# The first differential attention part issued head by head behind its own projections

## The chip, the cores and the metric

The kernel runs on one core of one Trainium2 chip. The metric is the device time of one execution in microseconds. A profile is one execution taken by the hardware profiler; its span runs from the first to the last instruction.

## The reference

One layer of a streaming encoder over 2048 prompt tokens and 32 sample tokens of width 1024. What the change touches is the projection and the differential attention of group A (4 heads; two query and key maps of 64 dimensions a head, values of 128):

```python
z = rmsnorm(x, g_attn) @ w_in            # q, k, v of group A, then of group B
s = einsum('bqhmd,bkhmd->bhmqk', q, k) * 64 ** -0.5 + bias[:, None]
p = softmax(where(mask, s, NEG))         # mask: chunks of 64, causal
w = p[:, :, 0] - lam * p[:, :, 1]
oa = einsum('bhqk,bkhe->bqhe', w, v)
```

Group B (8 heads of 64) attends to its own and the previous 8 chunks. Both groups are normed and joined, projected by `w_out` and added to the input. Then follow a squared-ReLU MLP of width 4096, a gate with a per-layer input p, and a final norm. Outputs are the tokens and all new keys and values.

## The kernel before

All matrix products are in fp32 parts: each operand is split into a high and a low part (`split`, L178: ScalarE or VectorE makes the high part, GpSimd or VectorE the low one), and `mm3` (L212) takes three matmuls for each product.

Tokens are handled in four blocks of 512 (the last one with the 32 sample tokens): blocks 0 and 1 are `HALVES[0]`, 2 and 3 `HALVES[1]`. For a block, `prep` (L359) loads the raw tokens, transposes them (tile xp) and makes the operands aH and aL; there is room for two blocks of them. `proj` (L438) computes values (tile vps, in `vtile`) and, for each of four head groups g, first queries and then keys (tile qps): one weight unit of 1024 x 128 (`wunit`, L189), and 24 matmuls for each block. VectorE takes the product out of PSUM (L476 for queries, L481 for keys), ScalarE and GpSimd split it into the tiles qh and ql, each in two buffers, and DMAs write them to HBM as qS and kS. New keys of group A are transposed back (tile ktp, L504), copied (kn) and written to the outputs. `prep_p` (L894) does the same to the per-layer input: transposes (ppt, L911), split into pph and ppl, which share the buffers of qh and ql, and DMAs to pS.

`attn_a` (L572) does attention A for a list js of query pairs (256 tokens each): for each head g it loads the bias tile ba, and a key tile ka with the keys up to the last pair, and calls `attn_a_pair` (L596) for each pair: a load of q, scores (tile s, L638), maximum and exponential (L644 to L652), the difference of the two maps (L674, L675), transposes (tpp, L713) with their split (L720, L721), the value products (tile o, L727 to L729), and the sub-norm (ss, L738). Scores go through three PSUM banks, transposes through two, o through one. The projection has a ring of two banks (pool mm). Pairs 0 to 3 are the first part (`JA0`), pairs 4 to 8 the second (`JA1`, much later). `attn_b` does attention B (scores sb, transposes tpb, products ob).

All DMAs are issued by SyncE (SP) in one line (`dma`, L152, L157). A DMA on SP that has to wait for another engine, or for an earlier DMA, holds those behind it. The order on each engine isn't the order of the calls: the tile framework places the instructions by their priority (the order of the calls, unless `lifted` raises it) and by a simulated time line, so that later work may stand between the instructions of earlier work as far as data, buffers and pools allow. Each engine then runs its own list in order.

In `run` the part around the change is, in the order of the calls: preparation of blocks 0 and 1 with group A's values; the bias tables (`lam`, `biases`); the queries and keys of group A for both blocks and all four heads, woven with `prep_p`, whose transposes and ktp go through the two banks of the attention's transposes; attention A for pairs 0 and 1 of all heads, then for pairs 2 and 3; group B's projection of block 0; that of block 1 woven with the preparation of block 2; attention B for pairs 0 to 3; group B's projection of block 2 woven with the preparation of block 3; and so on.

Of the kernel before, what the change touches and what calls it, by code (L numbers as in the profile page):

```python
# [42 lines left out]
HALVES = [(0, 1), (2, 3)]  # L43
# [29 lines left out]
GS = 3  # L73
OW = 1
KBW = 1184
JA0 = [(0, 1), (2, 3)]
JA1 = [(4, 5), (6, 7, 8)]
JB = [(0, 1), (2, 3), (4, 5), (6, 7, 8)]
ONP = (28, 1, 6)
# [4 lines left out]
def drain(gen):  # L84
    for _ in gen:
        pass
# [13 lines left out]
def weave(main, side, step, i=0, n=1):  # L100
    for _ in main:
        if i % step == 0:
            for _ in range(n):
                next(side, None)
        i += 1
    drain(side)
# [37 lines left out]
class Kern:  # L144
# [424 lines left out]
                    self.qS[gi, ms[0], :, j : j + n].rearrange("r k l c -> r (k l c)"),  # L569
                )  # L570

    def attn_a(self, js, pool, ps_s, ps_t, ps_o):  # L572
        nc = self.nc
        last = 8 in js
        nk = SP if last else 256 * (js[-1] + 1)
        late = []
        for g in range(4):
            ba = self.bias_a(pool, g)
            kt = pool.tile([P, 2, 1024 if self.small else SP], F32R, tag="ka", bufs=2, name="ka")
            if last:  # L580
                ks = pool.tile([P, 2, PAST + SS], F32R, tag="ks", bufs=1, name="ks")
            for hl in range(2):
                src = self.kS[g, hl].rearrange("(m r) c -> r m c", m=2)
                for c0 in range(0, nk, 1024):
                    c1 = min(c0 + 1024, nk)
                    self.dma(kt[64 * hl : 64 * hl + 64, :, c0:c1], src[:, :, c0:c1])
                if last:
                    self.dma(ks[64 * hl : 64 * hl + 64], src[:, :, SP:KC])
            for j in js:
                self.attn_a_pair(g, j if j < 8 else None, kt if j < 8 else ks, ba, pool, ps_s, ps_t, ps_o, late)  # L590
                if self.small:
                    late.pop(0)()
        while late:
            late.pop(0)()
# [861 lines left out]
    def run(self):  # L1456
        tc, nc, a = self.tc, self.nc, self.a
        with ExitStack() as top:

            def opened(stack, name, bufs, space=None, side="left"):  # L1460
                kw = {} if space is None else {"space": space}
                return stack.enter_context(
                    tc.tile_pool(name=name, bufs=bufs, side=side, reuse_waits="tile", **kw)
                )
# [7 lines left out]
            mm = opened(top, "mm", MM, PSUM)  # L1472
            tp = mm
            psx = ExitStack()
            ps_s = opened(psx, "pss", 5 - MM, PSUM, "right")
            ps_t = opened(psx, "pst", 2, PSUM, "right")
            ps_o = opened(psx, "pso", 1, PSUM, "right")
# [3 lines left out]
            sg = opened(s12, "sg", 2)  # L1481
            self.rb = {}
            with ExitStack() as x:
                pp = opened(x, "pp0", 3, side="right")
                wv = opened(x, "wv0", 1, side="right")
                acts = {b: self.actpair() for b in HALVES[0]}
# [15 lines left out]
                for b, i in todo:  # L1502
                    for c in range(2):
                        self.vtile(b, i, 0, c, units[c], acts, sg, mm)
                    next(gen, None)
            ppx = ExitStack()
            pp = opened(ppx, "pp", 1)
            self.rawp = Rings((self.wp, "wr"), (opened(ppx, "wr3", 1), "wr"))
            with ExitStack() as x:
                wk = opened(x, "setup", 1, side="right")  # L1510
                self.lam(cp, wk)
                self.biases(wk, ps_t)
                qk = self.proj(HALVES[0], 0, acts, sg, mm, Rings((ps_t, "tp")), vs=())
                weave(qk, self.prep_p(sg, wk, ps_t), 2)
            self.small = True
            mark = tc.tile_snap_priority()
            with ExitStack() as x:
                pool = opened(x, "a0", 1, side="right")
                for js in JA0:
                    self.attn_a(js, pool, ps_s, ps_t, ps_o)  # L1520
            drain(self.proj((0,), 1, acts, sg, mm, tp))

            def lifted(gen):
# [40 lines left out]
            with ExitStack() as x:  # L1564
                pool = opened(x, "a1", 1, side="right")
# [3 lines left out]
            wk = opened(sq_, "wk", 1)  # L1569
# [47 lines left out]
            wk = opened(top, "wk4", 1, side="right")  # L1617
# [6 lines left out]
            with ExitStack() as x:  # L1624
                act = Sized(opened(x, "acth", 2), BLK, True)
                weave(self.outproj(2, wk, oa[2], md, acc[2]), self.oload(3, wk, act, oa), 1, 0, 2)
                g = self.outproj(3, wk, oa[3], md, acc[3])
# [10 lines left out]
            g = self.gate(0, h, up, None, md, wk, made[0])  # L1638
# [11 lines left out]
            g = self.gate(2, h, up, None, md, wk)  # L1650
# [10 lines left out]
            g = self.gate(3, h, up, cs, md)  # L1661
# [50 lines left out]
```

## Time and profile before

| what | value |
|---|---|
| median of 3 runs | 3154.2 us (3153.26 to 3156.3) |
| span of the profiled execution | 3144.6 us |
| the median less the span | 9.6 us |
| granted TensorE clock over the span | 0.985 |
| TensorE busy | 3011.4 us, 96% |
| VectorE, ScalarE, GpSimd busy | 60%, 60%, 59% |

The profiled execution has no time of its own in the results; its span is set beside the median, and what lies around the span is taken to be 9.6 us. In the profile PE is TensorE's matmuls, PEld its weight loads, DVE VectorE, ACT ScalarE, POOL GpSimd and SP the queue of DMA issues. Matmuls overlap, so that the busy time of PE is a union of overlapping records. A row of a stretch gives its length, each engine's busy time with the count of its instructions, the granted clock, the mean busy share of the 16 DMA engines, and GB/s. A row of a wait gives who waited for whom, the total, how often, and the longest.

### The profile page before, as it was taken

The page shows a single profiled execution, that of the slowest core. Times are in us where ns is not written, and L with a number is a line of the kernel's source. Part 1 is how long each engine was busy: PE and PEld are TensorE (multiplying, and loading weights), DVE is VectorE, ACT ScalarE, POOL GpSimd, SP SyncE. Part 2 cuts the span into 40 slices and gives each one's busy share as a digit, 9 for nine tenths or more (in the row PEclk, how much of TensorE's full clock was granted, in tenths as well). Part 3 has the DMA queues.
Part 4 walks back from the last instruction along what each step waited for, and adds up shares of the span by engine and source line. Part 5 has one row for each costly group of instructions (what it writes and reads, how often), then busy time and mean ns, then how long its engine had stood idle before and what let it go on. Part 6 is the DMA issues. An engine that isn't in the chain of part 4 may idle for free. (4 is left out here: it accounts for less than half of the span.)

```text
span 3144.6 us, 52811 instructions
## 1 busy us (share of the span) xinstructions
PE 3011.4 (96%) x17913; PEld 2649.6 (84%) x17913; DVE 1897.6 (60%) x4596; ACT 1878.1 (60%) x4166; POOL 1847.6 (59%) x2496
## 2 busy tenths in 40 slices
PE   8999898999999999999999999999899999999998
PEld 7787786899977887878788888878788887999998
DVE  5157774645465654666756556535667885576653
ACT  6257775766676764776666656554555455554545
POOL 2357455332345644665655545667877888667674
PEclk9999999999999999999999999999999999999999
DMA  8788757986788746555564543437533446333231
GB/s 281 244 244 244 204 185 229 263 232 201 205 250 230 218 130 153 152 154 153 157 184 130 144 123 103 145 116 241 179 128 115 144 152 229 123 107 107 88 116 56
DMA packets 523287, 539.27 MB, mean 171 GB/s; under 512 B 38749, under 2 KB 401569, under 8 KB 523017
## 3 DMA queue, kind: packets, MB, share of 16 engines
q1 hardware_dynamic: 523016, 535.89, 57.5%
q8 instruction: 142, 2.33, 0.3%
q14 instruction: 129, 1.05, 0.1%
HBM read 421.97 MB, written 117.75 MB: 172 GB/s over the span
## 5 line engine op out<-in xcount | busy, mean ns | idle before, releaser
L176 POOL TENSOR_TENSOR wl<-wr,wh 128x256 fp32r<-128x256 f32 x648 | 475.6, 766 | 354.8 <-ACT wh L181 315.7
L181 ACT ACTIVATE piece<-wr 128x512 fp32r<-128x512 f32 x406 | 246.1, 626 | 272.7 <-PE ups L217 113.1
L176 POOL TENSOR_TENSOR piece<-wr,piece 128x256 fp32r<-128x256 f32 x404 | 327.4, 837 | 99.7 <-ACT piece L181 86.4
L181 ACT ACTIVATE wh<-wr 128x1024 fp32r<-128x1024 f32 x228 | 241.2, 1058 | 171.7 <-PE qps L217 40.7
L166 POOL TENSOR_TENSOR wl<-wr,wh 128x256 fp32r<-128x256 f32 x264 | 199.4, 787 | 194.1 <-ACT wh L181 183.9
L216 PE MATMUL dps<-uh,piece 128*128 128x272 f32 (+1 forms) x768 | 247.0, 325 | 7.5 <-ACT piece L181 3.2
L166 POOL TENSOR_TENSOR piece<-wr,piece 128x256 fp32r<-128x256 f32 x280 | 237.0, 878 | 26.9 <-ACT piece L181 21.5
L218 PE MATMUL dps<-uh,piece 128*128 128x272 f32 (+1 forms) x768 | 247.8, 325 | 1.6 <-POOL piece L166 1.3
L217 PE MATMUL dps<-ul,piece 128*128 128x272 f32 (+1 forms) x768 | 247.8, 323 | 0.0
L216 PE MATMUL ups<-cs,piece 128*128 128x256 f32 (+1 forms) x864 | 246.0, 285 | 1.0 <-DVE r L1232 1.0
L217 PE MATMUL ups<-cs,piece 128*128 128x256 f32 (+1 forms) x864 | 245.3, 284 | 0.0
L218 PE MATMUL ups<-cs,piece 128*128 128x256 f32 (+1 forms) x864 | 245.2, 284 | 0.0
L216 PE MATMUL qps<-aH,wh 128*128 128x512 f32 (+1 forms) x640 | 231.2, 361 | 7.3 <-ACT kn L506 4.0
L218 PE MATMUL qps<-aH,wl 128*128 128x512 f32 (+1 forms) x640 | 229.5, 359 | 0.0
L217 PE MATMUL qps<-aL,wh 128*128 128x512 f32 (+1 forms) x640 | 228.5, 357 | 0.0
L1173 DVE TENSOR_TENSOR h<-h,dps 128x512 f32<-128x512 f32 x256 | 174.3, 683 | 80.9 <-PE dps L218 75.4
L1221 DVE TENSOR_TENSOR h<-h,dps 128x272 f32<-128x272 f32 (+1 forms) x384 | 189.3, 515 | 51.8 <-PE dps L218 50.8
L216 PE MATMUL dps<-uh,wh 128*128 128x512 f32 x512 | 207.8, 406 | 9.4 <-DVE h L1173 5.7
L216 PE MATMUL ups<-cH,wh 128*128 128x512 f32 x512 | 202.8, 396 | 2.1 <-ACT cH L181 1.1
L638 PE MATMUL s<-ka,q 128*128 128x512 f32 (+3 forms) x768 | 187.2, 345 | 15.9 <-ACT e L652 7.1
L218 PE MATMUL dps<-uh,wl 128*128 128x512 f32 x512 | 201.7, 394 | 0.5 <-POOL wl L166 0.4
L217 PE MATMUL ups<-cL,wh 128*128 128x512 f32 x512 | 201.2, 393 | 0.0
(317 smaller groups left out, 9634.2 us busy)
## 6 DMA issues: line engine op xcount, KB each, us to landing
wr<-w_up SPq DMA_DIRECT2D x128, 512.0 KB, 4.0
wr<-w_down SPq DMA_DIRECT2D x128, 512.0 KB, 3.8
wr<-w_in SPq DMA_DIRECT2D x74, 512.0 KB, 5.1
q<-qS SPq DMA_DIRECT2D x128, 256.0 KB, 5.4
v<-vSa SPq DMA_DIRECT2D x64, 512.0 KB, 3.9
ka<-kS SPq DMA_DIRECT2D x32, 512.0 KB, 8.9
wr<-w_out SPq DMA_DIRECT2D x32, 512.0 KB, 4.7
wr<-w_ple_gate SPq DMA_DIRECT2D x32, 512.0 KB, 4.3
```

The source lines that it names most:

```text
L166: nc.gpsimd.tensor_tensor(out[:, sl], a[:, sl], b[:, sl], op=op)
L176: nc.gpsimd.tensor_tensor(out[:, sl], a[:, sl], b[:, sl], op=op)
L181: nc.scalar.activation(hi, raw, AF.Copy)
L216: nc.tensor.matmul(ps, lh, rh, start=start and i == 0, stop=False)
L217: nc.tensor.matmul(ps, lh, rl, start=False, stop=False)
L218: nc.tensor.matmul(ps, ll, rh, start=False, stop=stop and i == n - 1)
L638: nc.tensor.matmul(s, q[:, m, hl, P * qi : P * qi + nr], kt[:, m, k0 - kb : k0 - kb + n], start=hl == 0, stop=hl == 1)
L1173: nc.vector.tensor_tensor(hv, hv, ps, op=ALU.add)
L1221: nc.vector.tensor_tensor(hv, hv, ps, op=ALU.add)
```

## The change

Queries and keys of group A are no longer projected for all heads first. For each head g, `run` calls the projection of that head's queries and keys for both blocks, woven with two of the eight steps of `prep_p`, and then attention A of that head for the pairs 0 to 3. `attn_a` takes the heads as an argument, and `JA0` is one list of four pairs, so that a head loads its bias once, and one key tile of 1024 columns in place of one of 512 and one of 1024. The transposes of `prep_p` and ktp go through the ring of the projection's two banks. The pools of `prep_p`'s input and of the third weight buffer are opened inside this part, and the pool of the later preparations after it.

```diff
-JA0 = [(0, 1), (2, 3)]
+JA0 = (0, 1, 2, 3)
...
-    def attn_a(self, js, pool, ps_s, ps_t, ps_o):
+    def attn_a(self, js, pool, ps_s, ps_t, ps_o, gs=range(4)):
...
-        for g in range(4):
+        for g in gs:
...
-            ppx = ExitStack()
-            pp = opened(ppx, "pp", 1)
-            self.rawp = Rings((self.wp, "wr"), (opened(ppx, "wr3", 1), "wr"))
             with ExitStack() as x:
                 wk = opened(x, "setup", 1, side="right")
                 self.lam(cp, wk)
                 self.biases(wk, ps_t)
-                qk = self.proj(HALVES[0], 0, acts, sg, mm, Rings((ps_t, "tp")), vs=())
-                weave(qk, self.prep_p(sg, wk, ps_t), 2)
             self.small = True
             mark = tc.tile_snap_priority()
             with ExitStack() as x:
                 pool = opened(x, "a0", 1, side="right")
-                for js in JA0:
-                    self.attn_a(js, pool, ps_s, ps_t, ps_o)
+                pn = opened(x, "pn", 1)
+                self.rawp = Rings((self.wp, "wr"), (opened(x, "wr3", 1), "wr"))
+                rot = Rings((mm, "mm"))
+                pps = self.prep_p(sg, pn, rot)
+                for g in range(4):
+                    weave(self.proj(HALVES[0], 0, acts, sg, mm, rot, vs=(), gs=(g,)), islice(pps, 2), 2)
+                    self.attn_a(JA0, pool, ps_s, ps_t, ps_o, (g,))
+                drain(pps)
+            ppx = ExitStack()
+            pp = opened(ppx, "pp", 1)
+            self.rawp = Rings((self.wp, "wr"), (opened(ppx, "wr3", 1), "wr"))
             drain(self.proj((0,), 1, acts, sg, mm, tp))
```

## The prediction

> **What bounds the kernel now.** I read the page first, then the stretches of the part that the change moves, then who waits for whom in the stretches that lose time. The page says that TensorE is the engine of the whole span:
>
> ```profile
> span 3144.6 us, 52811 instructions
> PE 3011.4 (96%) x17913; PEld 2649.6 (84%) x17913; DVE 1897.6 (60%) x4596; ACT 1878.1 (60%) x4166; POOL 1847.6 (59%) x2496
> ```
>
> So a reordering can gain only where PE stands idle or runs at a lowered clock. I cut 62 to 640 us, where the moved work lies, by what PE does there: 62:180 is the query and key projection of group A, 180:480 the first part of attention A with the group B projection laid between its instructions, 480:640 the start of attention B. After length and engines' busy times come the granted clock, the share of the DMA engines and GB/s:
>
> ```profile
> core 0: us, PE busy (x) PEld busy (x) DVE busy (x) ACT busy (x) POOL busy (x), PEclk, DMA share, GB/s
> 62.00:180.00 118.00, 113.49 (x540) 89.23 (x539) 23.81 (x47) 27.54 (x46) 41.85 (x60) 0.97 0.72 236
> 180.00:220.00 40.00, 36.77 (x284) 34.80 (x283) 23.89 (x101) 25.04 (x80) 17.35 (x27) 1.00 0.91 252
> 220.00:280.00 60.00, 59.59 (x336) 51.24 (x335) 44.20 (x153) 42.97 (x129) 52.01 (x76) 1.00 0.94 258
> 280.00:380.00 100.00, 84.02 (x489) 74.17 (x488) 80.51 (x250) 74.26 (x229) 48.89 (x70) 0.86 0.76 215
> 380.00:420.00 40.00, 40.00 (x219) 34.60 (x218) 26.02 (x72) 28.39 (x76) 26.79 (x38) 1.00 0.64 194
> 420.00:480.00 60.00, 53.50 (x375) 48.85 (x374) 45.43 (x144) 44.99 (x131) 24.95 (x36) 0.94 0.56 173
> 480.00:560.00 80.00, 69.77 (x340) 56.48 (x339) 38.55 (x142) 49.05 (x124) 44.96 (x74) 0.94 0.84 241
> 560.00:640.00 80.00, 74.37 (x544) 70.77 (x544) 48.83 (x183) 59.22 (x136) 27.90 (x47) 0.96 0.91 259
> ```
>
> I count as PE's **shortfall** the length less busy time by clock: 7.9, 3.2, 0.4, 27.7, 0, 9.7, 14.4 and 8.6 us, in all 72.0 us. That is all there is to win here, if these matmuls don't run faster. Half of it lies in 280:380 and 420:480. The next rows show what is mixed there: score matmuls (s), transposes of raw tokens (xp, the preparation of blocks 2 and 3) and value projections; the vps row is of 180:220, the sb row (scores of attention B) of 480:560.
>
> ```profile
> 220.00:280.00 60.00, 12.01 (x63) 1.00 0.94 258
> 280.00:380.00 100.00, 21.27 (x82) 0.86 0.76 215
> 420.00:480.00 60.00, 8.90 (x36) 0.94 0.56 173
> 280.00:380.00 100.00, 3.63 (x24) 0.86 0.76 215
> 420.00:480.00 60.00, 3.60 (x24) 0.94 0.56 173
> 480.00:560.00 80.00, 2.11 (x16) 0.94 0.84 241
> 180.00:220.00 40.00, 26.41 (x183) 1.00 0.91 252
> 480.00:560.00 80.00, 10.09 (x42) 0.94 0.84 241
> ```
>
> The first three rows are s, the next three xp. In 220:280 attention runs at 63 s beside query and key projections and PE loses 0.4 us; in 280:380 it runs at 82 s beside value projections and xp, DVE is busy 80.51 of 100 us, and PE loses 27.7 us. So what loses is the partner, not attention. The waits of 280:380 (first two rows) and of 420:560 (the rest) agree:
>
> ```profile
> PE s L638 <- ACT e L652: 6.3, 6, 2.9
> PE s L638 <- DVE nm L647: 3.3, 4, 1.5
> PE rp L392 <- DVE xt L387: 4.4, 2, 2.8
> PE sb L835 <- DMA q<-qS: 3.1, 1, 3.1
> PE xp L378 <- DVE kr L481: 2.8, 1, 2.8
> ```
>
> **The change part by part.** The built programs have the same 17910 PE, 4598 DVE and 3589 ACT instructions; after has twelve loads fewer (eight of keys, 512 columns each, and four of the bias) and four memsets on POOL. These removals cost and save nothing on PE, since no wait for ka or ba stands among PE's. Everything else is order. In the instruction order of PE the first s moves from place 946 to 633 and the 256th (the last of this part) from 2457 to 2205; the last 7097 PE instructions are the same in both. I price after by giving each stretch of its order the shortfall of the stretch of before with the same mixture.
>
> (a) Places 457 to 1090: 384 query and key matmuls, as in 62:180, but 232 of them now among 82 s. The basis is 7.9 us. Three things come on top. First, head 0's keys go to HBM and come back while PE has only 67 instructions (55 of the projection, 12 transposes) to do. Here are the DMA rows, to landing, of 62:180 (first two) and of 180:480:
>
> ```profile
> kS<-qh SPq DMA_DIRECT2D x8, 256.0 KB, 3.9
> qS<-ql SPq DMA_DIRECT2D x8, 256.0 KB, 3.8
> kS<-ql SPq DMA_DIRECT2D x9, 256.0 KB, 6.7
> ka<-kS SPq DMA_DIRECT2D x8, 512.0 KB, 8.1
> ```
>
> and the rows of the projection's own chain in 62:180, DVE, DVE, DVE, ACT, POOL, PE:
>
> ```profile
> L915 DVE TENSOR_TENSOR ppl<-ppt,pph 128x512 fp32r<-128x512 f32 (+1 forms) x10 | 5.8, 591 | 24.0 <-ACT pph L914 10.0 <-DMA qS<-ql 8.7 <-DMA kS<-ql 5.3
> L481 DVE TENSOR_TENSOR kr<-qps,rbt 128x512 f32<-128x512 f32 x8 | 5.5, 691 | 25.5 <-PE qps L218 25.5
> L476 DVE SCALAR_TENSOR_TENSOR ql<-qps,rbt 128x512 f32<-128x512 f32 x8 | 5.5, 689 | 26.1 <-PE qps L218 11.4 <-PE ppt L911 7.3 <-DMA qS<-ql 5.2
> L181 ACT ACTIVATE qh<-kr 128x512 fp32r<-128x512 f32 x8 | 5.0, 630 | 15.4 <-DVE kr L481 9.1 <-DMA kS<-qh 4.0 <-DMA pS<-pph 2.2
> L166 POOL TENSOR_TENSOR ql<-kr,qh 128x256 fp32r<-128x256 f32 x14 | 10.1, 740 | 10.0 <-DMA pS<-ppl 6.2 <-issue 2.0 <-ACT qh L181 1.9
> L216 PE MATMUL qps<-aH,wh 128*128 128x512 f32 x128 | 52.0, 406 | 2.9 <-DVE ql L476 2.9
> ```
>
> DVE 0.69, ACT 0.63, POOL twice 0.74, the store 3.9 to 6.7 and the load 8.1 make 14.8 to 17.6 us. PE's cover is 67 instructions at 113.49/540, or 0.21 us each, 14.1 us. One stall of 0.7 to 3.5 us: I take 2, and for the range 0 to 9 (a second landing of 8.1 behind the first). The Trainium skill speaks against this step: "DMA: Bandwidth & Descriptors", section "Two DMAs through the same engine are not ordered", says that the issuing engine has to wait for the store's semaphore before it issues the load. In the order SP's load of ka indeed waits for the kS stores, so that every later DMA waits behind it; by the page's own fit in "Anatomy of one DMA" (2.0 us and bytes at 436 GB/s) store and load would make an estimated 5.8 us and the stall would vanish, by these rows it doesn't.
>
> Second, the transposes of the new keys and of the layer's inputs move into the two banks of the projection itself. One row of 60 to 640 has that wait, and the next counts the five ktp transposes around it in 560:640:
>
> ```profile
> PE qps L216 <- ACT kn L506: 4.0, 1, 4.0
> 560.00:640.00 80.00, 1.03 (x5) 0.96 0.91 259
> ```
>
> It occurs once where several groups use the bank; with eight groups of ktp after the change I take 2 us, bounds 0 and 8.
>
> Third, the two buffers qh and ql, through which queries, keys and layer inputs all go to HBM. Their waits for stores stand in the rows above: 8.7, 5.3 and 5.2 on DVE, 4.0 and 2.2 on ACT, 6.2 on POOL. Now only 2.9 us reach PE, because DVE is busy 23.81 of 118 us and has nothing else. After the change attention's DVE work queues behind the waiting instruction, and s waits for it. 232 of 384 matmuls lie in that stretch, and with attention beside them DVE is needed 44.20 of 60 us (220:280): 19.2 x 0.60 x 0.74 = 8.5 us. Bounds: 0 if the thinner stream of projections lets the stores land in time, 31.6 if all these waits reach PE. So (a) is 7.9 + 2 + 2 + 8.5 = 20.4.
>
> (b) Places 1090 to 1340, 169 value matmuls among 32 s, like 180:220 with 183: 3.2 x 169/183 = 3.0. (c) To 1700, query and key projections among 60 s, like 220:280: 0.4.
>
> (d) To 2110, block 1's values and block 2's preparation (24 xp) among 66 s, like 280:380 with 24 xp and 82 s: 27.7 x 66/82 = 22.3; bounds 15 and 33, since scores alone may not set it. (e) To 2380, projections among the last 16 s, like 380:420: 0.
>
> (f) To 2960, block 3's preparation (40 xp), which stood in 420:480 and 480:560, now all beside 86 sb and no s. The two stretches cost 9.7 + 14.4 = 24.1; they held 36 s and 42 sb, so 86 sb are a like load and I keep 24.1. Low bound 9.7, high bound 24.1 + 44 x 27.7/82 = 39, if each further sb costs what an s does in 280:380. (g) What follows is like 560:640: 8.6.
>
> Sum after: 20.4 + 3.0 + 0.4 + 22.3 + 0 + 24.1 + 8.6 = 78.8, against 72.0: **6.8 us more**. Later stages keep their partners (attention A's second part ends some 190 places earlier, beside the same MLP work), so I cost them at nothing; if that cover fails they add an unknown of either sign. The span is then 3151.4; the median of the runs, 3154.2, stands 9.6 above this span, so 3161.0.
>
> **Rivals.** *Thinner pairing (faster).* The preparation of block 3 no longer meets attention A's DVE load, and attention B, with two waits of its own in 420:560 at most, absorbs it: (f) falls to 9.7 and (d) to 15, the rings cost nothing: 72.0 becomes 7.9 + 4 + 3.0 + 0.4 + 15 + 9.7 + 8.6 = 48.6, so 3130.8; half of it 3143. For it: DVE and ACT are nearly idle in 62:180 and full in 280:380. Beside it stands the Trainium skill, "Perfetto Trace Analysis", section "Optimization Strategy": stages with different busiest engines may gain from being interleaved. In 220:280 the trace agrees. Against it: the full stretch itself stays in the order, as (d).
>
> *The store queue takes over (slower).* SP now issues loads of attention and stores of the projection in one line; a load that waits for a store, or for a buffer of q, holds the stores behind it, these hold qh and ql, and these hold DVE. A use of the pair is held 0.69 + 0.63 + 1.48 + SP's wait + 3.8, and the SP row of 62:180 says 1.6 each:
>
> ```profile
> SPq L157 <- ACT qh L181: 14.2, 9, 3.1
> ```
>
> That is 8.2 us. In (a) 24 uses (16 of q and k, 8 of layer inputs) come in some 140 us, two buffers allow 11.7 us each. From there on PE pays: with one ka landing of 8.1 in the hold it is 16.3, and if that befalls half of the 15 uses beside attention, 7.5 x (16.3 - 11.7)/2 = 17 us on top of the forecast: 3178.
>
> *It doesn't do what it says*: the order of before might already have had attention in the projection. The places 946 and 633 say no; 0.02, time as before.
>
> **How the numbers follow.** A measurement of this kernel tells about 0.2%, 6.3 us, from no change. Forecast as summed 0.41, of which 0.22 slower, 0.17 within, 0.02 faster; thinner pairing 0.31, faster; store queue 0.26, slower; no effect 0.02. That is faster 0.33, same 0.19, slower 0.48. The range reaches from three quarters of the first rival's gain (3154.2 - 17.5) to the second rival with half of the excess that the high bound of (f) allows (3178 + 7.5): 3137 to 3186.
>
> **What would show it.** The first s at about 101 us (176 places from 457 at 0.21 us, from 62 us, and the stall), and the last 252 places earlier than before, some 47 us (578 us for the 3127 instructions of the eight rows). (a): waits of DVE L476 and L915 for stores, with s behind them on PE. (d): the same s waits on ACT e and DVE nm around block 2's preparation. (f): sb and rp waits around block 3's. I am wrong if PE's shortfall up to the first third of attention B is under 60 us, or if the difference arises after 900 us, where I put nothing.

## The result and the profile after

| | before | after |
|---|---|---|
| median (lowest to highest, runs) | 3153.73 us (3149.46 to 3156.3, 4) | 3170.61 us (3168.97 to 3175.81, 4) |
| ratio, 95% interval | | 1.0067 [1.0055, 1.0078] |
| span of the profiled execution | 3144.6 us | 3168.5 us |
| granted clock over the span | 0.985 | 0.981 |

The change costs 16.9 us by the medians and 23.9 us by the two spans. The profiled execution of after took 3170.25 us, only 1.75 us more than its span. If the same holds for before, the execution that the prediction was built on took an estimated 3146 us and was one of the fastest: the 9.6 us that I put "around the span" are mostly the distance between that execution and the median. Both distances count below, medians where two kernels are compared, spans where stretches are.

The head of after's page, as the one shown of before: the same 17913 matmuls, longer.

```profile
span 3168.5 us, 52786 instructions
PE 3028.8 (96%) x17913; PEld 2660.1 (84%) x17913; DVE 1895.6 (60%) x4596; ACT 1880.5 (59%) x4166; POOL 1844.7 (58%) x2492
```

Next the stretches of after between the places 457, 1090, 1340, 1700, 2110, 2380, 2960 and 3300 of PE's order, which are the prediction's (a) to (g), in its columns (length, busy time of PE, PEld, DVE, ACT, POOL, granted clock, DMA share, GB/s):

```profile
75.00:217.00 142.00, 132.50 (x634) 104.93 (x635) 61.73 (x197) 64.81 (x177) 50.52 (x74) 0.94 0.77 235
217.00:249.00 32.00, 31.50 (x251) 30.18 (x250) 27.80 (x84) 25.76 (x75) 23.43 (x32) 1.00 0.77 231
249.00:315.00 66.00, 66.00 (x365) 56.90 (x365) 48.37 (x145) 47.32 (x129) 49.62 (x71) 1.00 0.78 227
315.00:385.00 70.00, 60.08 (x410) 54.97 (x409) 60.13 (x204) 57.16 (x182) 34.35 (x50) 0.90 0.63 186
385.00:439.00 54.00, 53.58 (x273) 44.66 (x272) 27.57 (x73) 31.63 (x79) 38.87 (x55) 1.00 0.58 188
439.00:563.00 124.00, 105.31 (x583) 89.36 (x581) 76.31 (x299) 87.79 (x236) 47.46 (x83) 0.90 0.88 248
563.00:626.00 63.00, 58.30 (x343) 50.67 (x343) 32.25 (x113) 39.79 (x82) 20.72 (x35) 0.92 0.75 218
```

Length less busy time by clock gives PE's shortfall: 17.5, 0.5, 0.0, 15.9, 0.4, 29.2 and 9.4 us, together 72.9, where I had forecast 78.8 and counted 72.0 of before. So between these two executions the part that the change moves costs almost nothing more, and most of the cost must lie outside it. One piece lies ahead of it. The first 75 us of before and of after:

```profile
0.00:75.00 75.00, 63.11 (x478) 59.13 (x479) 44.33 (x152) 46.82 (x142) 20.70 (x35) 1.00 0.90 284
```

```profile
0.00:75.00 75.00, 58.03 (x457) 55.46 (x457) 43.98 (x149) 45.96 (x136) 20.74 (x35) 1.00 0.92 294
```

That is 11.9 against 17.0 us of shortfall. The first 457 PE instructions are the same ones in both traces, but from the 60th on they don't start in the same order (the 60th is a transpose, xp, in before and a value product, vps, in after). In after the 457th ends at 72.7 us, in before at 70.3. What follows in after is the 458th, the first matmul of the bias tables (pa), which waits for its table ta to land; in before it stands later, at 77.4 us, and waits 1.6 us:

```profile
75.19 0.80 PE L297 MATMUL pa<-oa,ta 32*4 32x384 f32 x2 [2.45 <-DMA ta<-t_table]
```

So about half of the 5.1 us is this one wait, which the changed order of PE puts right behind place 457. The rest, 2.4 us, lies within the 457. SP's order differs there too. Its issues in the timeline (start, length) of before and of after:

```profile
8.81 1.06 SPq L157 DMA_DIRECT2D wr<-w_in  x2
9.92 2.95 SPq L157 DMA_DIRECT2D x<-x_prompt  x1
12.98 0.37 SPq L157 DMA_DIRECT2D wr<-w_in  x1
```

```profile
9.68 0.43 SPq L157 DMA_DIRECT2D pn<-p_prompt  x1
10.16 0.51 SPq L157 DMA_DIRECT2D wr<-w_in  x1
10.71 1.24 SPq L157 DMA_DIRECT2D pn<-p_prompt  x1
11.99 4.67 SPq L157 DMA_DIRECT2D wr<-w_in  x2
```

Two loads of the layer's inputs p (pn, 512 KB each), which before issues at 75 us, now stand between the first weight loads; their tiles come from a pool of their own. Of PE's waits of the first 76 us, before and then after, two grow most: the value matmuls wait longer for their weights, and pa for its table.

```profile
PE vps L216 <- ACT wh L181: 1.3, 1, 1.3
```

```profile
PE vps L216 <- ACT wh L181: 4.6, 2, 2.4
PE pa L297 <- DMA ta<-t_table: 2.4, 1, 2.4
```

The other piece lies late. These are the two stretches between the places 6600, 8600 and 10813 (from 10813 on PE's list is the same in both), where attention A's second part runs beside the MLP, first before, then after:

```profile
1167.00:1584.00 417.00, 400.42 (x2000) 334.42 (x1999) 267.42 (x604) 265.97 (x615) 238.34 (x327) 0.99 0.57 155
1584.00:2017.00 433.00, 426.65 (x2214) 360.12 (x2213) 252.25 (x569) 273.95 (x627) 236.95 (x343) 1.00 0.45 130
```

```profile
1172.00:1583.00 411.00, 396.04 (x2003) 331.53 (x2002) 268.55 (x595) 267.37 (x624) 238.82 (x323) 0.99 0.56 154
1583.00:2041.00 458.00, 443.05 (x2211) 371.44 (x2211) 259.22 (x559) 270.84 (x606) 256.64 (x369) 0.98 0.47 137
```

Before loses 20.6 + 6.3 = 26.9 us, after 18.9 + 23.8 = 42.7: +15.8, all in the second stretch, of which 8.6 is idle time (15.0 against 6.3) and the rest the clock of 0.98. PE's waits of after from 1584 to 2041 us name the partners, matmuls of the MLP (dps) behind ScalarE and VectorE:

```profile
PE dps L216 <- ACT relu L1138: 6.5, 3, 4.2
PE dps L216 <- DVE h L1173: 3.9, 3, 1.8
PE o L727 <- DMA v<-vSa: 2.7, 1, 2.7
```

In before the same stretch has this one row of dps, and none of relu:

```profile
PE dps L216 <- DVE h L1173: 1.6, 2, 1.3
```

The whole balance in shortfall, with stretches cut at the same places of PE's order in both traces (a clock is given to 0.01, so that a stretch of 400 us is known to some 2 us):

| places | before | after | difference |
|---|---|---|---|
| 0 to 457, with the wait of pa in after | 11.9 | 17.0 | +5.1 |
| 457 to 1090, (a) | 10.0 | 17.5 | +7.4 |
| 1090 to 1700, (b), (c) | 15.4 | 0.5 | -14.9 |
| 1700 to 2380, (d), (e) | 19.1 | 17.2 | -1.9 |
| 2380 to 2960, (f) | 20.6 | 29.1 | +8.4 |
| 2960 to 6600 | 25.4 | 25.7 | +0.2 |
| 6600 to 10813, second part of attention A | 27.1 | 44.2 | +17.1 |
| 10813 to the end | 47.1 | 47.3 | +0.2 |
| all | 176.7 | 198.4 | +21.6 of 23.9 |

(Long stretches were summed from shorter ones here, so that they differ by a few tenths from the rows above.) The moved work, 457 to 6600, comes out at -0.7.

How firm are these rows? Three of the complete kernels below keep before's order of PE up to place 6600 (experiments 8 and 9), and one keeps after's (experiment 9). Up to that place before lost 102.5 us, the three 101.4, 109.5 and 110.1; after lost 106.8, the other 106.1. So the early difference, 4.3 us, lies within what executions of one order differ by, and no early row under some 5 us can be read as a price by itself. Two rows do repeat: (a) lost 6.8 to 10.0 us with before's order and 16.2 and 17.5 with after's, (b) and (c) 15.0 to 15.8 and twice 0.5. The first stretch doesn't: the second kernel of experiment 8, with before's order, lost 16.9 us there, as much as after:

```profile
0.00:73.00 73.00, 59.02 (x457) 56.17 (x458) 43.90 (x148) 46.36 (x140) 20.99 (x35) 0.95 0.88 274
```

The late row, +17.1, is larger than that: in places 6600 to 10813 before lost 27.1 us and its second execution (experiment 8) 29.5. The question for the experiments is therefore double: what are the prices inside the start, which cancel, and is the late loss a consequence of the change or of the order that it happens to leave behind?

### The profile page after: what moved, and what is told of

It reads as the page before. It is cut to its first block, busy times and chain, and to the rows that moved or that the text cites. A ratio compares the mean times of both kernels' runs of the same rounds, so it can differ in the third digit from the quotient of the medians.

```text
span 3168.5 us, 52786 instructions
## 1 busy us (share of the span) xinstructions
PE 3028.8 (96%) x17913; PEld 2660.1 (84%) x17913; DVE 1895.6 (60%) x4596; ACT 1880.5 (59%) x4166; POOL 1844.7 (58%) x2492
## 5 line engine op out<-in xcount | busy, mean ns | idle before, releaser
L217 PE MATMUL dps<-ul,wh 128*128 128x512 f32 x512 | 204.5, 399 | 0.0
L218 PE MATMUL ups<-cH,wl 128*128 128x512 f32 x512 | 201.5, 394 | 0.0
```

What stands on the lines that cost most here:

```text
L217: nc.tensor.matmul(ps, lh, rl, start=False, stop=False)
L218: nc.tensor.matmul(ps, ll, rh, start=False, stop=stop and i == n - 1)
```

## The experiments

Theory at the outset: the head-by-head projection costs the start by its shared buffers (qh and ql, two banks), the rest follows. Rivals: the merged list of pairs does it, or the late loss is an accident of order.

**1. The merged list alone.** Before, with the four pairs in one list; all heads are still projected first.

```diff
-JA0 = [(0, 1), (2, 3)]
+JA0 = [(0, 1, 2, 3)]
```

> All heads are projected first, as before; only the two lists of pairs are merged, so that a head has one key tile and one bias load. Theory A (moving the projections between the heads is what costs, by the two qh and ql buffers and the round trip of the keys): the time stays with before, 3154 us within 6. Theory B (the merged list costs or gains by itself, in waits for the larger key tile or in what it meets later): it moves with the change, about 3170 us.

3166.4 us (3162.76 to 3170.48), ratio 1.0056 [1.0036, 1.0076]. Up to place 6600 its shortfall sums to 100.7 us, before's to 102.5; after it to 97.4 against 74.2. The late stretches of this kernel:

```profile
1163.00:1590.00 427.00, 401.53 (x2005) 336.39 (x2005) 276.12 (x600) 265.81 (x612) 241.95 (x322) 0.97 0.54 147
1590.00:2026.00 436.00, 430.97 (x2211) 362.55 (x2210) 246.42 (x560) 270.64 (x624) 243.78 (x358) 1.00 0.46 135
```

Here the first stretch loses 37.5 us and the second 5.0, the reverse of after. A kernel without any moved projection has a late price of the same size (42.5 us in the two stretches, after's 42.7) in another place. The theory that only the moved projection costs falls.

**2. Head by head with two key tiles.** The change without its merged list.

```diff
-                    self.attn_a(JA0, pool, ps_s, ps_t, ps_o, (g,))
+                    for js in (JA0[:2], JA0[2:]):
+                        self.attn_a(js, pool, ps_s, ps_t, ps_o, (g,))
```

> Projections head by head as in the change, but each head's attention in two lists of two pairs, with two key tiles (512 and 1024 columns) and two bias loads. Theory A (moving the projections costs): about 3170 us, as the change. Theory B (the merged list costs): about 3154 us, as before.

3180.37 us (3179.44 to 3184.02), ratio 1.0098 [1.0081, 1.0115]: 125.0 us of shortfall up to place 6600 and 84.8 after it. Neither theory had this time. Without the merged list the start costs 18 us more than after's 106.8. One of SP's waits from 62 to 400 us fits that, this kernel and then after:

```profile
SPq L157 <- PE s L638: 35.4, 20, 4.5
```

```profile
SPq L157 <- PE s L638: 21.9, 13, 4.2
```

A load that waits until the scores release a buffer holds every DMA behind it, 20 times instead of 13. That the 18 us of PE come from there is argued from these rows, not shown. What the times show is that the two parts of the change can't be added up: the ratio is 1.0056 for the merged list alone, 1.0098 for the loop over the heads alone, and 1.0067 for both.

**3. p after the last head.** The changed kernel, with `prep_p` taken out of the head loop; it runs when that has ended.

```diff
-                    weave(self.proj(HALVES[0], 0, acts, sg, mm, rot, vs=(), gs=(g,)), islice(pps, 2), 2)
+                    drain(self.proj(HALVES[0], 0, acts, sg, mm, rot, vs=(), gs=(g,)))
```

> The change, with the eight steps of the layer input's preparation called after the last head instead of two beside each head, so that qh and ql serve queries and keys alone while the heads are projected. Theory of the two buffers: PE's shortfall up to the end of the projection falls by the 8.5 us of the prediction, the time to about 3162 us. Rival (the buffers don't bind, the loss lies later): 3170 us within 5.

3186.98 us (3181.89 to 3197.56), ratio 1.0121 [1.0096, 1.0146]. Its stretches of the places 457 to 1090 and 1090 to 1340:

```profile
76.00:207.00 131.00, 126.74 (x634) 102.15 (x634) 59.70 (x193) 62.16 (x170) 53.99 (x78) 0.97 0.75 222
207.00:255.00 48.00, 38.37 (x255) 34.17 (x255) 37.90 (x125) 39.96 (x122) 21.23 (x31) 0.93 0.88 265
```

(a) falls from 17.5 to 8.1 us, before's level: p is worth 9.4 there, where I had put 8.5 on the buffers. (The edit moves all of p's work, its transposes in the projection's banks too, so that the buffers aren't separated from the rest of p.) But the next stretch, where p now lies beside attention, loses 12.3 against 0.5. The price belongs to p and goes where p goes. The time, 16.4 us above after's, fits neither theory: 13 us more than in after are lost between the places 2960 and 6600 (38.6 against 25.7 us), where neither had put anything.

**4. p ahead of head 0.** The same step at the other end: `prep_p` in one go, then the heads.

```diff
                 pps = self.prep_p(sg, pn, rot)
+                drain(pps)
                 for g in range(4):
-                    weave(self.proj(HALVES[0], 0, acts, sg, mm, rot, vs=(), gs=(g,)), islice(pps, 2), 2)
+                    drain(self.proj(HALVES[0], 0, acts, sg, mm, rot, vs=(), gs=(g,)))
```

> The changed kernel with the per-layer input p prepared in one go ahead of head 0, so that only queries and keys share the two buffers qh and ql with attention. Theory A (the rings cost the start: three kinds of stores share two buffers while attention waits behind them on VectorE): PE's shortfall of the first 60% of the projection's places falls from 17.5 us by about 8, the price that I gave the buffers, and nothing comes back after it, since p is done: about 3162 us. Theory B (p isn't the cause; the first scores wait for the round trip of the keys and for the doubled load of VectorE): the start keeps its price, and the first score comes some 15 us later for p's 96 transposes: 3170 or more. In the run with p behind the last head the start fell by 9 and 17 us came back.

3190.91 us (3188.39 to 3193.57), ratio 1.0123 [1.0103, 1.0142]; inside theory B's "3170 or more", but for the reason of neither theory. (The first s comes at 158.2 us, 30 later than in after and not 15, and p has 34 transposes in PE's records, not 96.) Its stretches of the places 457 to 1090 and 1090 to 1700, and PE's largest wait from 62 to 270 us:

```profile
77.00:235.00 158.00, 129.58 (x635) 103.49 (x636) 61.86 (x191) 66.43 (x172) 56.65 (x83) 0.89 0.71 214
235.00:330.00 95.00, 95.00 (x609) 86.08 (x608) 67.30 (x212) 68.30 (x192) 64.75 (x92) 1.00 0.77 229
```

```profile
PE ppt L911 <- DVE ppl L915: 24.3, 4, 11.2
```

Alone, p stops PE for 24.3 us in four waits. The timeline shows what the longest is made of: PE waits for VectorE, VectorE for ScalarE, and ScalarE for a store of the buffer to land. The last two rows, of SP, are from the same stretch:

```profile
104.17 0.60 ACT L914 ACTIVATE pph<-ppt 128x512 fp32r<-128x512 f32 x1 [11.72 <-DMA pS<-pph]
104.83 0.69 DVE L915 TENSOR_TENSOR ppl<-ppt,pph 128x512 fp32r<-128x512 f32 x1 [11.63 <-ACT pph L914]
105.58 1.12 PE L911 MATMUL ppt<-ident,pn 128*128 128x128 f32 x4 [11.21 <-DVE ppl L915]
90.27 5.02 SPq L157 DMA_DIRECT2D dbb<-rb  x8
95.39 0.59 SPq L157 DMA_DIRECT2D pS<-pph  x1
```

That store is issued only at 95.39 us, behind eight DMAs of the bias tables (dbb) that hold SP from 90.27 us on, and it lands some 8.7 us later. So the buffer ring is a real price, and p pays it: 34.6 us in one go (42.7 less the 8.1 that (a) costs without p), 9.4 among the projections, 11.8 beside attention. The 34.6 aren't the ring's alone, since p in this place also meets the bias tables on SP. Of the three placements the change has the cheapest. What follows p here, 95 us of projections and attention, loses nothing.

**5. The projection one head ahead of attention.**

```diff
-                for g in range(4):
-                    weave(self.proj(HALVES[0], 0, acts, sg, mm, rot, vs=(), gs=(g,)), islice(pps, 2), 2)
-                    self.attn_a(JA0, pool, ps_s, ps_t, ps_o, (g,))
+                for g in range(5):
+                    if g < 4:
+                        weave(self.proj(HALVES[0], 0, acts, sg, mm, rot, vs=(), gs=(g,)), islice(pps, 2), 2)
+                    if g > 0:
+                        self.attn_a(JA0, pool, ps_s, ps_t, ps_o, (g - 1,))
```

> The changed kernel with the projection one head ahead: heads 0 and 1 projected, attention 0, head 2 projected, attention 1, and so on. The order of PE changes only a little, because the scheduler lays the projection between attention in any case. Theory A (head 0's round trip of keys through HBM is a price): the stalls of PE around 100 us (1.97 us for ql) and of the first score go, 2 to 4 us less: about 3167 us. Theory B (the start's price is buffers and VectorE, not the round trip): within 3 us of the changed kernel up to attention B, and what the order of the rest rolls decides: 3165 to 3185.

3175.36 us (3170.61 to 3176.39), ratio 1.007 [1.0051, 1.0089], after's own. Theory A's gain isn't there: (a) loses 21.4 us, after's 17.5. Theory B's time holds, but not its 3 us up to attention B: up to place 2380 the shortfall is 64.3 us, after's 52.1. The round trip of head 0's keys was no price that could be saved in after. In other orders a wait for keys does show: PE's scores wait for ka 2.2 us in experiment 2, 1.2 in experiment 4 and 7.2 in experiment 6.

**6. The transposes through attention's banks.** The ring that before used, now with attention on it.

```diff
-                rot = Rings((mm, "mm"))
+                rot = Rings((ps_t, "tp"))
```

> The change, with the transposes of the new keys and of the layer input through the two banks of attention's transposes, as before the change, instead of the projection's own ring. If the projection's banks cost what the prediction put on them (2 us, at most 8): 3162 to 3168 us. If the transposes of attention now wait behind them instead: 3170 us or more.

3267.06 us (3264.88 to 3271.02), ratio 1.0373 [1.0355, 1.0391]. Its stretches of the places 457 to 1090 and 1090 to 1700, and two of PE's waits from 62 to 400 us:

```profile
78.00:250.00 172.00, 138.94 (x636) 111.11 (x635) 78.80 (x268) 78.57 (x232) 52.33 (x76) 0.87 0.54 160
250.00:402.00 152.00, 110.88 (x612) 95.95 (x611) 78.40 (x260) 80.59 (x233) 60.08 (x88) 0.83 0.60 174
```

```profile
PE tpp L713 <- DVE e L675: 19.0, 13, 3.2
PE qps L216 <- DVE ql L476: 15.0, 3, 6.6
```

51.1 and 60.0 us are lost, well beyond the "3170 us or more" of the second expectation. The rows fit a simple account, which no further run tests: each transpose that waits for its data now holds a bank that attention needs, and the other way round. Moving ktp and ppt to the projection's banks isn't a price of the change but its condition: I had put it at a cost of 2.

**7. Without attention A's second part.** Both kernels leave out pairs 4 to 8 of attention A and write zeros in their place, so that the tokens from 1024 on are computed from these zeros and the times stand only beside each other.

```diff
-                for js in JA1:
-                    self.attn_a(js, pool, ps_s, ps_t, ps_o)
+                zt = pool.tile([P, T - 1024], F32, name="zt")
+                nc.gpsimd.memset(zt, 0.0)
+                for g in range(4):
+                    self.dma(self.oT[:, g, 1024:T], zt)
```

> The kernel before without the second part of attention A (pairs 4 to 8 and the sample tokens of group A are left out, zeros stand in their place). It is the partner of the next run. No theory sets its own time; it serves as the base of the next one.

> The changed kernel without the second part of attention A (the same part left out). Theory early (the change costs in what it reorders, up to the end of attention B): the difference to the cut kernel before stays at the full 17 us or more. Theory late (much of the cost arises where attention A's second part, now some 190 places earlier, stands among the MLP's products): the difference falls to about 10 us or less.

Before's form took 2917.11 us (2912.47 to 2918.2), after's 2924.51 (2923.92 to 2930.02); as ratios to before 0.9254 [0.9238, 0.9271] and 0.9276 [0.9259, 0.9293]. The change costs 7.4 us of medians here, where it costs 16.9 in the whole kernel, as theory late had it ("about 10 us or less"). Some 9.5 us of it don't appear without attention A's second part. The 7.4 that are left lie in part early: in the profiled executions, 17.5 us apart, PE reaches place 5400 at 934.0 us instead of 922.8. That is near the 6.8 forecast for the moved part, but two executions that are the slowest and the fastest of their kernels can't confirm it.

**8. Before once more, and before with another late order.** The first is the unchanged kernel; the second changes one parameter of the weaving in the last blocks, which moves PE's order from place 7407 on only.

```diff
-ONQ = (8, 1, 1)
+ONQ = (10, 1, 1)
```

> The kernel before once more, for a second profile: how far the shortfall of a stretch differs between two executions of one program. If stretches repeat within 1 us and the span within 3, the differences between before and the change by stretch can be read as they stand; if the first 75 us differ by 5, their 5 us in the change is of the execution and not of the change.

> The kernel before with one parameter moved that changes PE's order only from place 7407 on (the norm of group B's outputs starts two steps of the MLP later, same work). Theory accident (attention A's second part and the MLP in before stand in a lucky phase and any other phase costs): 5 to 12 us slower than before, all of it after 1250 us. Rival (the late order is not sensitive): before's time within 3 us.

3149.8 us (3147.8 to 3156.1), ratio 0.9997 [0.9986, 1.0007], and 3150.04 us (3143.1 to 3156.52), ratio 0.9995 [0.9986, 1.0005]. The two spans of before differ by 2.6 us, but their stretches don't repeat within 1 us: the first loses 14.0 instead of 11.9, (a) 6.8 instead of 10.0. The shortfall from place 6600 on is 77.9 and 76.6 us, against 74.2. This nudge doesn't roll the late loss anew; taken alone it speaks against the theory of an accident.

**9. The late order rolled in both kernels.** The second part of attention A in one list, in before and in after: the same edit, far behind the change.

```diff
-JA1 = [(4, 5), (6, 7, 8)]
+JA1 = [(4, 5, 6, 7, 8)]
```

> The kernel before with the second part of attention A in one list of pairs 4 to 8 for each head; the first part and everything up to it as before. Theory A (the late part's loss is an accident of the order in which attention A's second part meets the MLP): any result from 3140 to 3185, the part up to the first MLP within 3 us of before, and the difference all in the second part. Theory B (merged lists are better or worse as such because the key tile is loaded once a head): the late loss falls, since two large key loads a head become one, to 3145 or less. Merging the first part alone gave 3166, with the loss late.

> The changed kernel with the second part of attention A in one list too. To be set beside the kernel before with the same edit. Theory A (the part of the change's cost that arises late is an accident of order): the late difference of this pair isn't the some 14 us of the unmerged pair but any value between -15 and +20, and the early difference stays at some 8 us. Theory B (the change leaves something behind that costs the second part, whatever its order): the late difference is +10 to +17 again and this kernel stands 17 to 24 us above its partner.

| second part | without the change | with the change |
|---|---|---|
| two lists | 3153.73 us | 3170.61 us, 1.0067 [1.0055, 1.0078] |
| one list | 3161.45 us (3155.91 to 3169.9, 10 runs), 1.0028 [1.0015, 1.0042] | 3153.8 us (3148.89 to 3162.04, 10 runs), 1.0004 [0.9988, 1.0019] |

The ratios stand to before. With the late part in one list the changed kernel is 7.7 us *below* its partner (8.3 by the means, 95% interval 3.8 to 12.9), with two lists 16.9 above. The late stretches (places 6600, 8600, 10813) without and then with the change:

```profile
1174.00:1601.00 427.00, 403.55 (x2002) 335.75 (x2001) 263.86 (x574) 264.10 (x600) 237.33 (x320) 0.97 0.50 142
1601.00:2036.00 435.00, 428.24 (x2215) 362.58 (x2214) 263.80 (x597) 278.81 (x640) 242.25 (x344) 1.00 0.42 122
```

```profile
1173.00:1584.00 411.00, 395.29 (x2001) 331.04 (x2000) 259.60 (x568) 259.01 (x596) 233.01 (x319) 0.99 0.52 147
1584.00:2025.00 441.00, 433.77 (x2215) 364.38 (x2214) 263.90 (x586) 279.49 (x633) 254.39 (x368) 1.00 0.44 134
```

They lose 35.6 + 6.8 = 42.4 us and 19.7 + 7.2 = 26.9. These are about after's 42.7 and before's 26.9 with the kernels exchanged, though the large loss lies in the first of the two stretches here and in the second there. (The profiled execution of the first took 3169.07 us, 7.6 above its median, that of the second 3152.16, 1.6 below; the medians leave about half of the difference.) Up to place 6600 the changed kernel loses 106.1 us, after's 106.8, and its partner 110.1 with before's order; so the "some 8 us" of an early difference that I had expected aren't seen between these two executions, nor is the first kernel within 3 us of before's 102.5 there. The late difference, -15.5, lies at the edge of the range that theory A gave the pair. For the first kernel by itself theory B (3145 or less) fails. The theory that the change leaves something behind that costs the second part in any order falls as well. What remains is that the change shifts attention A's pairs against the MLP's matmuls, and that the rest of the order decides whether they meet well; that is a reading of these four times, and no run shows the single wait behind it.

No complete version beats before by more than its interval.

## Why the prediction was right or wrong

The direction and the range held; the size, +6.8 forecast and +16.9 measured, did not. The time, 3170.61 us, lies between the forecast, 3161, and the second rival, 3178. That the direction held was in part luck: between the two profiled executions the moved part, priced at 78.8 against 72.0 us, came out at 72.9, and most of the difference arose late, where the sum has nothing and where the same change gains beside another order. Point by point:

- **"Later stages keep their partners ... so I cost them at nothing"** is the step that failed. The shortfall of the places 6600 to 10813 went from 27.1 to 44.2 us. The clause behind it ("an unknown of either sign") was right: experiment 9 shows -15.5 between the profiled executions for the same change beside another late order. I had named the unknown and given it no width. Half of the measured 16.9 us doesn't appear without that part (experiment 7).
- **What lies ahead of place 457** had no term. The 457 instructions end at 72.7 us instead of 70.3, and pa behind them then waits 2.45 us. Over all uncut kernels the end lies between 72.7 and 75.3 us in the seven with the head loop and between 70.3 and 73.3 in the five without it, 2.4 us apart on the average. The matmuls wait for weights 3.1 to 6.2 us in the seven and 1.3 to 2.6 in the five. The two early loads of p fit that by their place, but PE's own order differs there too, and no run held the loads back alone, so that this cause is argued, not shown. I had priced PE's order from place 457 on and nothing ahead of it.
- **(a)** forecast 20.4, measured 17.5, or 19.9 with the wait of pa just ahead of it, for which I had no term. The largest one on top of the basis, 8.5 for the buffers qh and ql, has about the size that experiment 3 finds for p as a whole (9.4). One of its stalls can be read in after's timeline, VectorE behind a store and PE behind VectorE:

```profile
101.20 0.69 DVE L476 SCALAR_TENSOR_TENSOR ql<-qps,rbt 128x512 f32<-128x512 f32 x1 [1.94 <-DMA qS<-ql]
101.95 0.50 PE L216 MATMUL qps<-aH,wh 128*128 128x512 f32 x1 [1.97 <-DVE ql L476]
```

  The 2 us for the first round trip of the keys were not there: PE's waits of after from 62 to 270 us have no row for ka, and experiment 5 gains nothing. The first s came at 128.0 us, not 101; I had counted from 62 us where the stretch behind place 457 begins at 75.2, and at 0.21 us a matmul where the 181 instructions of 75 to 128 us, mostly of 512 columns, have 47.2 us of busy time (0.26 each) and 5.8 of idle time; part of the busy time ran at a lowered clock:

```profile
75.00:101.00 26.00, 23.66 (x89) 14.66 (x89) 4.57 (x9) 2.65 (x4) 4.26 (x6) 0.93 0.65 209
101.00:128.00 27.00, 23.54 (x92) 18.22 (x93) 3.46 (x6) 6.60 (x10) 9.08 (x14) 0.87 1.00 311
```

  By the fit of the Trainium skill ("DMA: Bandwidth & Descriptors", section "Anatomy of one DMA"), which the page gives for DMAs issued through GpSimd while these go through SyncE, that stall was to vanish. It did, but not by the fit's times: from 75 to 217 us the loads of ka (512 KB) took a median of 6.3 us and the stores of ql to kS (256 KB) 5.9, where the fit gives an estimated 3.2 and 2.6. What covered them was the longer way to the first s.
- **(b), (c), (e)** forecast 3.4 and 0, measured 0.5 and 0.4: a stretch took its loss from its partners, as the sum assumed. Attention beside projections loses nothing (249:315). The Trainium skill's advice in "Perfetto Trace Analysis", section "Optimization Strategy", to interleave stages with different busiest engines, fits that stretch; for the whole kernel no gain came of it.
- **(d)** 15.9 against 22.3, at the low bound; **(f)** 29.2 against 24.1, inside its bounds of 9.7 and 39. The waits of 439 to 563 us are the ones named, sb and rp:

```profile
PE sb L835 <- DMA q<-qS: 5.5, 3, 3.3
PE sb L835 <- DVE stb L838: 3.9, 5, 1.3
PE rp L392 <- DVE xt L387: 3.8, 2, 3.3
```

- **The rivals.** Thinner pairing was half right: the last s comes at 403.2 us, 51 earlier, and (b) to (e) lose less, but (f) and the start take it back. The store queue didn't take over in the changed kernel, where (a) stayed under its forecast; experiment 2, with SP's longer waits, may be such a case.
- **What would show me wrong** was a shortfall under 60 us up to the first third of attention B, which was 72.9, or a difference that arises after 900 us. The second came: 17 of 22 us between the profiled executions.

Open: which wait starts the late loss. The rows name relu, h and v in after, while the merged list alone loses in the other stretch; no run held the early part and moved single pairs of the second one.

## What to carry to other kernels

Compare the instruction lists of every engine and of the DMA queue from the first line on, not only of the bound engine from the place where the moved work begins: here two loads of p went ahead of weights that are needed sooner. Where a scheduler lays two stages into each other, an early edit shifts them against each other later. Give that an own width in the range (here the same change came out 16.9 us above and 7.7 us below its partner, of 3150), and before keeping or dropping such a change, measure it beside a second late order. Profile each kernel more than once before stretches are compared. Where a ring of two buffers is emptied by stores, spread the work that shares it: p cost 9.4 us spread among the projections and 34.6 gathered ahead of them.

## What the runs showed of the hardware

- Executions of one and the same program differ more than three or four of them show: before took 3144.06 to 3165.47 us in 19 runs of one series, 0.7%.
- The granted clock differs between stretches: 0.93 and 0.87 in 75 to 128 us of after, in the second of which PE was busy 23.54 of 27 us and the DMA engines all of the time; in the 66 us from 249 on, without idle time, it was 1.00. In the late stretch of after (1583:2041) the clock of 0.98 cost 8.9 us beside 15.0 of idle time, about half of what that stretch lost more than before's.
- With p alone on the ring, ScalarE waited up to 11.7 us for a buffer (the row of experiment 4), though the stores of 256 KB took a median of 4.7 (pph) and 6.0 us (ppl) to land in after. Some 3 us of that wait passed before the store was issued, behind eight other DMAs on SP, and the store then took some 8.7 us to land.
